# A delta-rule layer whose weight blocks come as two halves: head 1 to 7 by two GpSimd transfers and one ScalarE negative, in place of one transfer, one cast and one subtraction

## The chip, the cores and the metric

The kernel runs on one core of a Trainium2 chip. A core has five engines that run side by side, each through its own fixed list of instructions: TensorE (PE in the profile, with PEld for its weight loads), VectorE (DVE), ScalarE (ACT), GpSimd (POOL) and SyncE (SP, which here only issues transfers). Transfers run on 16 DMA engines; they are issued by SP into hardware queues, or by POOL into a software queue. The metric is the time of one execution on the device in microseconds (us), the median of several runs. The kernel before takes 1331.79 us (3 runs, 1331.76 to 1331.99).

## The reference

The reference is an encoder of two layers on x (1 x 512 x 1024), all in float32: a gated delta-rule layer, an MLP, a gated linear attention layer, an MLP, with a layer norm after each. Only the first of them is touched. Cut to that layer:

```python
def _mixer_gdn(h, w_in, conv_w, a_log, dt_bias, norm_g, w_out):
    proj = jnp.matmul(h, w_in).astype(F32)
    qkv = jax.nn.silu(_depthwise_conv(proj[..., :A_CONV_CH], conv_w.astype(F32)))
    z = proj[..., A_CONV_CH:A_CONV_CH + A_VW]
...
    q = _l2norm(heads(qkv[..., :A_W], A_DK)) * (A_DK ** -0.5)
    k = _l2norm(heads(qkv[..., A_W:2 * A_W], A_DK))
    v = heads(qkv[..., 2 * A_W:], A_DV)
...
    o_f = _gated_delta_chunked(q, k, v, beta[0], g[0])
    o_b = _flip(_gated_delta_chunked(_flip(q), _flip(k), _flip(v), _flip(beta[1]), _flip(g[1])))
    o = (o_f + o_b).transpose(0, 2, 1, 3)
    o = _rmsnorm(o, norm_g) * jax.nn.silu(z.reshape(bn, s, A_HEADS, A_DV))
    return jnp.matmul(o.reshape(bn, s, A_VW).astype(w_out.dtype), w_out)
```

There are 8 heads of width 128, so the projection has, for each head, four column blocks of w_in: k, q, v and z, each 1024 x 128.

## The kernel before, in words

**Three products for one.** A float32 matrix product is made from halves in a reduced format (fp32r in the profile): each operand is split into a high part, the value rounded to that format, and a low part, the rest. `mm3` (L122, L123, L124) adds high by high, low by high and high by low. A weight block is 128 x 1024 in the core's memory (8 slices of 128 rows of w_in side by side), and its projection is 24 matmuls of 128 x 512: L122, L123 and L124 for each of the 8 slices. The activations' halves xth and xtl are made once at the start and kept.

**How a weight block comes in before.** `wcols` (L104 to L111) takes a buffer `wst`, has SP load the block into it from device memory (`dma`, L50), and calls `split` (L84 to L102): ACT casts `wst` to the high part `wh` (L96), and DVE subtracts, `wl` = `wst` - `wh` (L101). The pool `wst` has 3 buffers; the pool `whl` has 3 buffers of `wh` and 3 of `wl`. So block n can be cast when the matmuls of block n-3 have read their halves, while the load into `wst` runs up to three blocks ahead of that.

`split` has another way (`by_dma`, L97 to L99), used at a few places of later stages: ACT writes the negative of the source into the low part, and a POOL transfer with an add accumulates a second copy onto it.

**Order.** `GdnHead.project` (from L1408) makes the four blocks of a head in the order k, q, v, z, and behind each the short convolution (`conv`, L1395 on ACT and L1399 four times on DVE) or, for z, a copy (L1434); behind q stands a silu over two or four tiles (L1437, with an activation table load ahead, and one behind at L55). `rows` (from L1446) transposes k and q (`ktp`, L1457, PE), copies the transposed k to `kt` (L1460), sums squares (`junk`, L1462, eight of them), takes the logarithm (`lnr`, L1465, ACT), makes scale factors on DVE and ACT (L1472 to L1498; `neg`, `kds`, `fq` on ACT), and has PE transpose the rows `rsp` to `rtp` (L1483). Then `solve` (the triangular inverse: `ep`, `kk`, `hp`, `lv`, `nw`, `xp`), `recur` (the two chunked recurrences: `m`, `op`) and `finish` (norm, gate, transpose) follow. The head's parts are generators: while head i projects, head i-1 solves and head i-2 recurs and finishes. A scheduler that models the engines draws from them and sets a fixed list for each engine; at run time every engine goes through its list in order, and an instruction that waits holds up all that stand behind it on the same engine. Priorities come out of the model, so an instruction that the model thinks late or early moves the others too.

Head 0 is special: its k block is loaded with the first transfers of the program, and its other three are issued early. While head 0 projects, POOL is still making masks (`blk`, `ic`, `icc`, `self`, `sel`, L1163 to L1205).

Of the kernel before, what the change touches and what calls it, by code (L numbers as in the profile page):

```python
# [8 lines left out]
F32 = mybir.dt.float32  # L9
F32R = mybir.dt.float32r  # L10
# [3 lines left out]
ALU = mybir.AluOpType  # L14
# [3 lines left out]
P = 128  # L18
# [10 lines left out]
class Ctx:  # L29
# [74 lines left out]
    def wcols(self, w, c0, n=P, pool=None, late=(), by_dma=False):  # L104

        st = self.wst.tile([P, KT, n], F32, name="wst", tag="wst")
        self.dma(st, w[c0 // n])
        with contextlib.ExitStack() as es:
            for i in late:
                es.enter_context(self.tc.issue_after(i.ins))  # L110
            return self.split(st, [P, KT, n], pool, by_dma)  # L111

    def wrows(self, w, r0, c0, pool=None):

        st = self.wst.tile([P, 2, 512], F32, name="wst", tag="wst")
        self.dma(st, w[r0 // (2 * P), c0 // 512])
        return self.split(st, [P, 2, 512], pool)
# [1253 lines left out]
class GdnHead:  # L1371
# [35 lines left out]
    def project(self, done):  # L1407

        c, pool, g, h = self.c, self.pool, self.g, self.h
        A = c.nc.scalar  # L1410
        if h == 0:
            self.new_tile()
        kq = self.kq
        for i, ci in enumerate((A_H + h, h, 2 * A_H + h, 3 * A_H + h)):
            if h == 0 and i == 0:
                ps = g.k0
            else:
                with g.then() if h == 0 else contextlib.nullcontext():
                    wh, wl = c.wcols(self.w_in, ci * P)
                ps = c.bank([P, S], F32, name="pj" + "kqvz"[i], tag="pj")  # L1420
                for k in range(KT):
                    c.mm3(ps, wh[:, k, :], wl[:, k, :], c.xth[:, k, :], c.xtl[:, k, :], k == 0, k == KT - 1)
                    if h == 0 and (i, k) == (3, 6):
                        g.sums()
                        yield from rows
                    if k < KT - 1:
                        yield 0.69, 0.0
            if i == 2:
                vz = self.next.new_tile()
                self.v, self.sz = vz[:, 0, :], vz[:, 1, :]  # L1430
            if i < 3:
                self.conv(kq[:, i, :] if i < 2 else self.v, ps, ci)
            else:
                A.copy(self.sz, ps)  # L1434
            if i == 1 or i == 3 and h == A_H - 1:
                t = vz if i == 3 else self.sil if h else kq
                c.exp_ln_after(A.activation(t, t, AF.Silu))  # L1437
            yield 0.69, 0.0
            if i == 1:
                rows = self.rows(done)  # L1440
                if h:
                    yield from rows
                else:
                    next(rows)
                    next(rows)
# [384 lines left out]
```

## Time and profile before

The profiled execution is one run out of several; its span is the time from its first to its last instruction.

| What | Value |
|---|---|
| median of 3 runs | 1331.79 us (1331.76 to 1331.99) |
| the profiled execution, its own time | 1330.95 us |
| its span | 1329.0 us |
| mean granted TensorE clock | 0.997 |
| delta-rule layer in the span | about 0 to 375 us, heads 1 to 7 projected from 37.5 to 333.3 us |

The profile's page gives, for each engine, busy time, share of the span and number of instructions, then the chain of work that ended last, then groups of instructions. A stage of the kernel is read from the view by windows: busy time of each engine in a stretch, the clock, the share of the 16 DMA engines in use, and GB/s. The timeline lists single instructions: start, duration, engine, line, output <- input, and in brackets the idle time ahead of it on that engine with what ended it. Matmuls overlap in PE's pipeline, so the time that one costs is the distance of two starts, not its duration.

### The profile page before, as it was taken

Reading aid. Unit: us, or ns where it says so; the run is one execution under the profiler, and the core shown is the slowest. Engines: PE = TensorE matmul, PEld = TensorE weight load, DVE = VectorE, ACT = ScalarE, POOL = GpSimd, SP = SyncE. Lnnn points to the kernel's source line nnn. Section 1 sums busy time; section 2 is a strip of 40 time slices with the busy share of each in tenths; the row PEclk is TensorE's granted clock in tenths of the full one; section 3 lists DMA queues with packets and bytes.
Section 4 is the critical chain, followed back from the end, with each engine's and each line's share of the span. In section 5 each row is a group of like instructions: output and inputs, shape, how many; then the busy total and the mean of one; then the engine's idle time right before and its main releaser. Section 6 shows DMA issues by size and latency. Waiting matters only on the chain.

```text
span 1329.0 us, 22303 instructions
## 1 busy us (share of the span) xinstructions
PE 1310.3 (99%) x8659; PEld 1120.2 (84%) x8659; DVE 1108.9 (83%) x1818; ACT 805.3 (61%) x1598; POOL 124.7 (9%) x177
## 2 busy tenths in 40 slices
PE   9999999999999999999999999999999999999996
PEld 7777877777877889999998888888889899999985
DVE  7787888878768988989988787867878789889888
ACT  4757666767643666566667754554466466566656
POOL 5000000000001810101101200000001001101011
PEclk9999999999999999999999999999999999999998
DMA  5210110111232574575548521211217365556465
GB/s 182 95 49 33 55 59 34 63 49 56 73 112 96 176 179 153 145 196 152 149 146 169 154 85 64 75 53 64 96 63 226 94 196 151 146 172 157 145 140 145
DMA packets 44044, 154.35 MB, mean 116 GB/s; under 512 B 5419, under 2 KB 5795, under 8 KB 43939
## 3 DMA queue, kind: packets, MB, share of 16 engines
q1 hardware_dynamic: 32163, 110.85, 24.6%
q0 software_dynamic: 11776, 42.08, 15.9%
q8 instruction: 68, 1.11, 0.3%
q14 instruction: 37, 0.30, 0.1%
HBM read 113.99 MB, written 2.10 MB: 87 GB/s over the span
## 4 chain that ended last, share of the span: by engine, by line
PE 92%; DVE 4%; ACT 3%; issue 1%; DVEq 0%; POOL 0%; ACTq 0%; POOLq 0%
PE fx L124 3%; PE fx L123 3%; PE fx L122 3%; PE pX L123 3%; PE pX L122 3%; PE pX L124 3%; PE pjv L122 3%; PE pjv L123 3%; PE pjv L124 3%; PE m L1692 3%; PE fyz L124 3%; PE fyz L122 3%; PE fyz L123 3%; PE pY L123 2%; PE pY L122 2%; PE pY L124 2%
## 5 line engine op out<-in xcount | busy, mean ns | idle before, releaser
L96 ACT CAST wh<-wst 128x1024 fp32r<-128x1024 f32 x152 | 159.5, 1049 | 115.9 <-PE fyz L123 38.2
L101 DVE TENSOR_TENSOR wl<-wst,wh 128x1024 fp32r<-128x1024 f32 x150 | 184.7, 1232 | 46.1 <-ACT wh L96 45.3
L101 DVE TENSOR_TENSOR w2l<-w2r,w2h 128x1024 fp32r<-128x1024 f32 x92 | 112.5, 1223 | 22.2 <-ACT w2h L96 22.2
L96 ACT CAST w2h<-w2r 128x1024 fp32r<-128x1024 f32 x94 | 98.4, 1048 | 45.1 <-PE pX L124 16.7
L400 POOL DMA_DIRECT2D w2r<-w2r x56 | 48.5, 896 | 497.4 <-DVE w2l L101 252.9
L96 ACT CAST ah<-h 128x1024 fp32r<-128x1024 f32 x56 | 58.9, 1051 | 40.4 <-PE pX L123 18.3
L448 DVE TENSOR_TENSOR wst<-wst 128x512 f32<-128x512 f32 x120 | 80.0, 688 | 0.4
L101 DVE TENSOR_TENSOR al<-h,ah 128x1024 fp32r<-128x1024 f32 x56 | 68.5, 1223 | 4.4 <-ACT ah L96 4.4
L123 PE MATMUL pX<-w2l,ah 128*128 128x512 f32 x168 | 66.2, 394 | 0.0
L122 PE MATMUL pX<-w2h,ah 128*128 128x512 f32 x168 | 66.1, 393 | 0.0
L124 PE MATMUL pX<-w2h,al 128*128 128x512 f32 x168 | 65.7, 391 | 0.0
L122 PE MATMUL pjv<-wh,xth 128*128 128x512 f32 x128 | 54.4, 425 | 0.0
L124 PE MATMUL fx<-xh,wl 128*128 128x256 f32 x192 | 54.3, 283 | 0.0
L124 PE MATMUL fyz<-xh,wl 128*128 128x256 f32 x192 | 54.2, 282 | 0.0
L122 PE MATMUL fx<-xth,wh 128*128 128x256 f32 x192 | 54.2, 282 | 0.0
L124 PE MATMUL fx<-xth,wl 128*128 128x256 f32 x192 | 54.2, 282 | 0.0
L123 PE MATMUL fx<-xtl,wh 128*128 128x256 f32 x192 | 54.2, 282 | 0.0
L122 PE MATMUL fyz<-xh,wh 128*128 128x256 f32 x192 | 54.2, 282 | 0.0
L123 PE MATMUL fx<-xl,wh 128*128 128x256 f32 x192 | 54.1, 282 | 0.0
L123 PE MATMUL fyz<-xl,wh 128*128 128x256 f32 x192 | 54.0, 281 | 0.0
L122 PE MATMUL fx<-xh,wh 128*128 128x256 f32 x192 | 53.8, 280 | 0.0
L123 PE MATMUL pj<-xtl,wh 128*128 128x256 f32 (+1 forms) x160 | 52.2, 328 | 0.2 <-DVE xtl L188 0.2
(536 smaller groups left out, 4326.2 us busy)
## 6 DMA issues: line engine op xcount, KB each, us to landing
wst<-in_w SPq DMA_DIRECT2D x68, 512.0 KB, 4.3
w2r<-in_w SPq DMA_DIRECT2D x60, 512.0 KB, 3.8
w2r<-w2r POOLq DMA_DIRECT2D x56, 512.0 KB, 5.3
wst<-in_a_in SPq DMA_DIRECT2D x32, 512.0 KB, 3.3
wst<-in_b_vr SPq DMA_DIRECT2D x16, 512.0 KB, 3.4
wst<-in_a_out SPq DMA_DIRECT2D x8, 512.0 KB, 3.3
wst<-in_b_in SPq DMA_DIRECT2D x8, 512.0 KB, 3.4
wst<-in_b_out SPq DMA_DIRECT2D x8, 512.0 KB, 3.3
```

The costliest lines, as they stand in the source:

```text
L96: h = nc.scalar.copy(hi, src)
L101: self.halves = h, nc.vector.tensor_tensor(lo, src, hi.bitcast(F32), ALU.subtract)
L122: mm(ps, ah, bh, start=start, stop=False, **kw)
L123: mm(ps, ah, bl, start=False, stop=False, **kw)
L124: self.last_mm = mm(ps, al, bh, start=False, stop=stop, **kw)
L400: nc.gpsimd.dma_start(blocks[a + (q,)], blocks[b + (q,)], accum_op=ALU.add)
L448: plus = lambda a, b: V.tensor_tensor(a, a, b, ALU.add)
L1692: T.matmul(ps[:, d, :], *ops(d), start=True, stop=True)
```

## The change

A new function `wcast` makes the two halves without `wst`: POOL issues a transfer from device memory into `wh` whose type is fp32r, so the transfer rounds; ACT writes the negative of `wh` into `wl`; POOL issues a second transfer of the same block from device memory, which adds to `wl`. `project` uses it for the blocks of heads 1 to 7 (28 blocks); head 0 keeps `wcols`. The lines behind it move down by 9: L1395 becomes L1404, and so on; `mm3` becomes L131 to L133.

```diff
+    def wcast(self, src):
+
+        nc = self.nc
+        hi, lo = (self.whl.tile(list(src.shape), F32R, name=n, tag=n) for n in ("wh", "wl"))
+        nc.gpsimd.dma_start(hi, src)
+        nc.scalar.mul(lo, hi.bitcast(F32), -1.0)
+        nc.gpsimd.dma_start(lo, src, accum_op=ALU.add)
+        return hi, lo
...
@@ GdnHead.project
                 with g.then() if h == 0 else contextlib.nullcontext():
-                    wh, wl = c.wcols(self.w_in, ci * P)
+                    wh, wl = c.wcast(self.w_in[ci]) if h else c.wcols(self.w_in, ci * P)
                 ps = c.bank([P, S], F32, name="pj" + "kqvz"[i], tag="pj")
```

The lists of the engines change at many places, since the scheduler is run anew. SP loses 28 loads, DVE loses 28 subtractions, ACT has 28 negatives in place of 28 casts, POOL gains 56 transfers, PE has the same matmuls in a slightly other order. Behind the delta-rule layer the lists are the same but for small shifts near its end. Two places are shown.

**The first block of head 1.** POOL's list before, at the end of its masks (`ic`, `icc`, `self` and `sel` are masks; the next row belongs to the layer norm at the end of the layer):

```order
L1203 TENSOR_TENSOR ic<-ic 128x4
L1205 CAST icc<-ic 128x4
L1163 MEMSET self 6x256
L1165 AFFINE_SELECT self<-self 6x256 x3
L1168 CAST sel<-self 6x256
L213 DMA lnp<-in_ln_g 128x512 x2
```

And in the changed kernel at the same place:

```order
L1212 TENSOR_TENSOR ic<-ic 128x4
L1214 CAST icc<-ic 128x4
L117 DMA wh<-in_a_in 128x1024
L1172 MEMSET self 6x256
L1174 AFFINE_SELECT self<-self 6x256 x3
L1177 CAST sel<-self 6x256
L119 DMA wl<-in_a_in 128x1024
L117 DMA wh<-in_a_in 128x1024 x2
L119 DMA wl<-in_a_in 128x1024 x2
```

The first transfer of a high part stands behind the mask `icc`, and the first of a low part behind the mask `sel`; from there on high and low alternate, at four spots two and two as in the last two rows.

ACT's list before, while head 0 projects (`ge` is of the gates, `sil` holds what the convolutions make, the third row is head 1's first block):

```order
L1279 ACTIVATE ge<-ge 128x128
L96 CAST wh<-wst 128x1024
L1395 ACTIVATE sil<-pjq,cw 128x512
L1437 ACT_TABLE_LOAD
L1437 ACTIVATE sil<-sil 128x1024
L55 ACT_TABLE_LOAD
L1460 COPY kt<-ktp 128x512
```

And in the changed kernel:

```order
L1288 ACTIVATE ge<-ge 128x128
L1404 ACTIVATE sil<-pjq,cw 128x512
L118 ACTIVATE wl<-wh 128x1024
L1446 ACT_TABLE_LOAD
L1446 ACTIVATE sil<-sil 128x1024
L55 ACT_TABLE_LOAD
L1469 COPY kt<-ktp 128x512
```

The negative of head 1's k block stands directly ahead of the table load and the silu of head 0, behind whose result head 0's transposes `ktp` stand on PE; the cast that it replaces stood one row further up.

On PE, behind the end of head 0's z projection, the second group of `ktp` stands behind 5 matmuls of head 1's k block (6 before), and `rtp` behind 18 of them (24 before).

**Head 2's rows, while head 3 projects.** ACT's list before (`ssp` gets the sums of squares that `lnr` takes, `pjz` is the z projection of head 2, `oss` belongs to head 1's finish, `pz` to head 2's solve):

```order
L96 CAST wh<-wst 128x1024
L1740 ACTIVATE junk,oss<-op 128x128
L1462 ACTIVATE junk,ssp<-ktp 128x128 x4
L96 CAST wh<-wst 128x1024
L1465 ACTIVATE lnr<-ssp,bias_77 128x8
L1434 COPY sil<-pjz 128x512
L1612 CAST pz_135<-lv 32x4x32 x4
L1489 ACTIVATE neg<-rw 128x8
```

And in the changed kernel:

```order
L118 ACTIVATE wl<-wh 128x1024
L1443 COPY sil<-pjz 128x512
L1749 ACTIVATE junk,oss<-op 128x128
L1471 ACTIVATE junk,ssp<-ktp 128x128 x2
L118 ACTIVATE wl<-wh 128x1024
L1471 ACTIVATE junk,ssp<-ktp 128x128 x2
L205 ACTIVATE rsy<-oss,bias_77 128x4
L1474 ACTIVATE lnr<-ssp,bias_77 128x8
L206 ACTIVATE rsy<-rsy 128x4
L1498 ACTIVATE neg<-rw 128x8
```

The negative of head 3's v block (the second L118) stands ahead of the last two sums of squares and of `lnr`, and the `pz` casts of the solve, which stood between `lnr` and `neg`, stand further up.

PE's list before, ahead of the `rtp` of head 2 (`ath`, `Dd` and `lv` belong to head 2's solve):

```order
L1598 LDWEIGHTS ath
L1598 MATMUL lv<-Dd,ath 128x64
L122 MATMUL pjk<-xth,wh 128x512
L123 MATMUL pjk<-xtl,wh 128x512
L124 MATMUL pjk<-xth,wl 128x512
L1483 LDWEIGHTS rsp
L1483 MATMUL rtp<-idb,rsp 6x128
```

And in the changed kernel:

```order
L132 MATMUL pjk<-xtl,wh 128x512
L133 MATMUL pjk<-xth,wl 128x512
L131 MATMUL pjk<-xth,wh 128x512
L132 MATMUL pjk<-xtl,wh 128x512
L1492 LDWEIGHTS rsp
L1492 MATMUL rtp<-idb,rsp 6x128
```

In the changed kernel the `lv` products of head 2 stand earlier, ahead of the end of head 2's z projection. From the last matmul of that projection to `rtp` there are now 4 transposes `ktp`, 4 products `qk`, 8 products `nw` and 17 projection matmuls of head 3's k block.

## The prediction

> **What bounds the kernel now.** I read first the engines' shares and the chain that ended last, on the page:
>
> ```profile
> PE 1310.3 (99%) x8659; PEld 1120.2 (84%) x8659; DVE 1108.9 (83%) x1818; ACT 805.3 (61%) x1598; POOL 124.7 (9%) x177
> PE 92%; DVE 4%; ACT 3%; issue 1%; DVEq 0%; POOL 0%; ACTq 0%; POOLq 0%
> ```
>
> PE sets the end. The change lies in the delta-rule layer, so the view by windows comes next, for the start, the stretch where heads 1 to 7 project, and the end of the layer (PE, PEld, DVE, ACT, POOL busy, clock, DMA share, GB/s):
>
> ```profile
> 0.00:36.00 36.00, 33.82 (x166) 27.79 (x166) 26.16 (x52) 18.89 (x28) 17.25 (x47) 1.00 0.52 181
> 36.00:330.00 294.00, 291.42 (x2543) 231.43 (x2542) 245.56 (x514) 198.70 (x564) 0.00 (x0) 1.00 0.16 54
> ```
>
> From 36 to 330 us PE is idle for 294.00 - 291.42 = **2.6 us**, at full clock, with the DMA engines at 16%. Nothing else is full: DVE has 48 us to spare, ACT 95, POOL does nothing. So whatever the change takes off DVE or SP can win little, and whatever makes PE wait counts in full. What PE waits for in this layer (us, times, longest):
>
> ```profile
> PE lv L1598 <- ACT pz L1612: 1.7, 6, 0.4
> PE nw L1644 <- ACT Dd L1633: 0.8, 2, 0.6
> PE ktp L1457 <- ACT sil L1437: 0.7, 1, 0.7
> PE ktp L1457 <- ACT junk L1462: 0.4, 1, 0.4
> ```
>
> PE waits for ACT, never for a weight. Against the durations that PE's matmuls have at their closest spacing the layer also holds a few us more that no row names; I count them neither way.
>
> **The change part by part.** Removed from DVE, and what ACT's cast waits for now (us, times):
>
> ```profile
> L101 DVE TENSOR_TENSOR wl<-wst,wh x28: 1209/1218/1227, 39.5 to 315.9; 128x1024 fp32r<-128x1024 f32 x28
> ...
> L96 ACT CAST wh<-wst x29: 1034/1047/1137, 35.9 to 327.7; 128x1024 fp32r<-128x1024 f32 x29
> its engine sat idle before it (us, times) until:
>   PE pjv L123: 9.4, 3
>   PE pjk L123: 7.7, 5
> ```
>
> DVE is relieved of 28 x 1.218 = 34.1 us. PE's 2.6 us of idle is the most that this can return; its named waits are for ACT, which feeds on DVE at one remove, so I take **-1.0** (bounds 0 and -2.6). PE has the same matmuls, in an order with 12 fewer changes between a projection and something else. A matmul of 128x512 costs 0.23 us behind its like and 0.31 behind another kind (starts 39.25, 39.56, 39.79 below), so 12 x 0.08 = **-1.0**.
>
> ACT keeps an instruction of the same length: the negative takes what the cast took (the row of a like one below, 1051 against 1047 ns). But the cast waited only until PE freed a buffer, since its `wst` had landed long before; the rows above show it standing for PE, 9.4 and 7.7 us in all, at no cost to PE. The negative waits until PE frees the buffer **and** a POOL transfer into it has landed. ACT stands longer by one landing, with all that is queued behind the negative. That is the price to size. Landings of 512 KB (median us from issue), the POOL instruction that issues one, and a negative of the same shape:
>
> ```profile
> wst<-in_a_in SPq DMA_DIRECT2D x32, 512.0 KB, 3.3
> w2r<-w2r POOLq DMA_DIRECT2D x56, 512.0 KB, 5.3
> wl<-wst POOLq DMA_DIRECT2D x2, 512.0 KB, 4.9
> ln<-in_ln_b POOLq DMA_DIRECT2D x2, 512.0 KB, 4.1
> ...
> L400 POOL DMA_DIRECT2D w2r<-w2r x56: 847/859/1245, 460.8 to 1285.2; - x56
> ...
> L98 ACT ACTIVATE wl<-wst x2: 1048/1051/1054, 731.3 to 738.2; 128x1024 fp32r<-128x1024 f32 x2
> ```
>
> No row shows a rounding transfer. Plain ones from SP take 3.3, accumulating ones of POOL 5.3, a plain one of POOL from device memory 4.1. The last is the nearest, same queue and same source, so the landing is **4.1**, with 3.3 and 5.3 kept as ends. In a sentence apart: the Trainium skill, page "DMA: Bandwidth & Descriptors", section "Anatomy of one DMA — SWDGE (gpsimd) path", fits 2.0 us plus bytes over 436 GB/s to a POOL transfer, an estimate of 3.2 us for 512 KB; the trace's 4.1 to 5.3 doesn't agree, and by 3.2 each place below would cost 0.9 less.
>
> The weights themselves come in time. A block's buffer is free when the block three before it ends; landing, negative, second landing are 4.1 + 1.05 + 4.9 = 10 us, and the blocks themselves start 13 us (head 1) to 28 us after that (starts of `pjk`, `pjq`, `pjv`, `pjz` in the timeline). L124, the only reader of `wl`, comes third. So PE should wait for ACT, not for weights.
>
> **Term 1, the start.** POOL, ACT and PE in the timeline:
>
> ```profile
> 28.42 0.19 POOL L1205 CAST icc<-ic 128x4 f16<-128x4 f32 x1
> ...
> 30.69 1.28 ACT L1437 ACT_TABLE_LOAD   x1 [4.73 <-DVE sil L1399]
> 31.98 1.06 ACT L1437 ACTIVATE sil<-sil 128x1024 f32<-128x1024 f32 x1
> 41.19 0.30 ACT L1465 ACTIVATE lnr<-ssp,bias 128x8 f32<-128x8 f32 x1
> ...
> 33.09 0.66 PE L1457 MATMUL ktp<-ident,sil 128*128 128x128 f32 x4 [0.65 <-ACT sil L1437]
> 43.53 0.39 PE L1483 MATMUL rtp<-idb,rsp 128*6 128x128 bf16 x4
> ```
>
> Head 1's first transfer stands behind `icc`, so it is issued at 28.6 and lands at 32.7; the negative ends at 33.8, the table load and the silu 1.28 + 1.06 later at 36.1. PE's `ktp`, which waits for that silu already, started at 33.09 with the silu's end at 33.04. **+3.1** (3.3: +2.3; 5.3: +4.3). Nothing on PE can slip in: in PE's list `ktp` keeps its place.
>
> **Term 2, head 0's rows.** In PE's new list `rtp` of head 0 stands behind 18 matmuls of head 1's k block in place of 24, the second `ktp` behind 5 in place of 6. From F, the end of head 0's z projection, PE has 18 matmuls and a `ktp` to `rtp`: 18 x 0.23 + 2 x 0.08 + 0.36 = 4.7 us. The second `ktp` is done at F + 1.6, its four sums of squares and `egl` put `lnr` at F + 3.5, and from `lnr` to the last row cast on DVE it is 43.12 - 41.19 = 1.9 (rows above and below): F + 5.4. PE waits 0.7 to 0.9: **+0.8**. The negative of head 1's v block stands behind `lnr`; it ends at F + 0.2 + 4.1 + 1.05 = F + 5.4, and `neg`, `kds`, `fq` (0.65) bring ACT to `rt` at F + 6.0, when `rtp` is done too: nothing more at 4.1, up to 1.2 at 5.3.
>
> ```profile
> 42.95 0.17 DVE L1480 CAST rsp<-r 128x8 bf16<-128x8 f32 x1
> ```
>
> **Term 3, the later heads.** The costliest place is head 2's rows, where the negative of head 3's v block now stands among the sums of squares. Let F be the end of head 2's z projection on PE. ACT: landing 4.1, negative 1.05, two sums of squares of 0.40 (starts 39.99, 40.40), `rsy` 0.3, and the 1.9 from `lnr` to the last row cast: 8.2 us. PE from F to `rtp`: 4 `ktp` 0.36, 4 `qk` 1.0, 8 `nw` 0.46, 17 matmuls 17 x 0.23 + 2 x 0.08 = 4.1: 5.9 us.
>
> ```profile
> 38.89 0.60 PE L1457 MATMUL ktp<-ident,sil 128*128 128x128 f32 x4
> 39.25 0.47 PE L122 MATMUL pjk<-xth,wh 128*128 128x512 f32 x1
> 39.56 0.39 PE L123 MATMUL pjk<-xtl,wh 128*128 128x512 f32 x1
> 39.79 0.39 PE L124 MATMUL pjk<-xth,wl 128*128 128x512 f32 x1
> ...
> 120.50 1.16 PE L1651 MATMUL qk<-sil 128*128 128x128 f32 x8
> 121.50 0.38 PE L1750 MATMUL otp<-ident,fo 128*128 128x128 f32 x2
> ...
> 122.38 0.39 PE L1666 MATMUL nw<-Xd,a 128*128 128x128 f16 x4
> 122.61 0.44 PE L1512 MATMUL kk<-sil 128*128 128x128 f32 x2
> ...
> 39.99 0.28 ACT L1462 ACTIVATE junk<-ktp 128x128 f32<-128x128 f32 x1
> ...
> 40.40 0.27 ACT L1462 ACTIVATE junk<-ktp 128x128 f32<-128x128 f32 x1
> ```
>
> PE waits 2.3 us. Without the landing ACT would still need `ktp` from PE (done at F + 1.9), all four sums (1.6), the negative, `rsy` and the 1.9, together 6.7, so 0.8 of it comes from the new order; at the later heads the order makes such tight spots and removes others, and I charge only what the landing adds, 8.2 - 6.7 = **1.5**. The same sum at the other 25 blocks, each with the instructions between the negative and the next ACT result that PE waits for, gives 0 at 19, and at six 1.15 (q of head 4), 0.3 (v of 4), 1.1 (v of 5), 0.8 (k of 6), 0.7 (q of 6) and 0.6 (v of 6), together **4.7**; these six are estimates, from rows of the same kinds as those shown. At 3.3 the seven places shrink to about 2.5 in all; at 5.3 each costs 1.2 more, and a few new ones appear: about 17.
>
> **The sum.** 3.1 + 0.8 + 1.5 + 4.7 - 1.0 - 1.0 = **+8.1 us**. The profiled execution took 1330.95 with a span of 1329.0, so it would be 1339.1; the runs' median is 0.8 above it, and the forecast for a median is **1340**. The ends of the unknown landing: 3.3 gives 2.3 + 0.8 + 2.5 - 2 = +3.6, 1335, and a DVE relief at its bound, -2.6, 1334; 5.3 gives 4.3 + 2.0 + 17 - 1 = +22, 1354.
>
> **The rivals.**
>
> (A) *The waits are hidden and the relief counts* (the other side). ACT has 95 us to spare, and the order that I read row by row may let PE run on while ACT stands. Then only the gains stay: -1.0 and at most -2.6, so 1328 to 1331. It decides if the first rounding transfer lands by 29.6, since then the silu isn't late; at 28.6 issued, no row has a landing that short. Against it too: PE's four rows of waits are all for ACT.
>
> (B) *A rounding transfer lands like an accumulating one or later.* Each word is changed on the way, as in an accumulation, and two POOL transfers of one block share the queue. At 5.3 or more it is the upper end, 1350 to 1356. For it speaks that the accumulating rows are the only ones of POOL that do arithmetic; against it, that DMA is at 16% here.
>
> (C) *POOL issues late.* If DVE holds POOL up while it writes a transfer's descriptors, each place is late by that: the 56 issues of the row above take 847 to 1245 ns beside a DVE as busy as here, so at most 0.4 us at the seven places and the start, +3.2, 1343. The Trainium skill, page "SBUF — State Buffer", section "Who interferes with whom", says that DVE in a two-port mode fully blocks GpSimd, and that a POOL transfer can starve so; the median of 859 against a least of 847 shows almost none of it here.
>
> (D) *The transfer doesn't round.* Then `wl` would be zero, with the same instructions and waits: the time is that of the forecast.
>
> **How the numbers follow.** A measurement of this kernel can tell about 0.2%, 2.7 us, from no change: faster is below 1329.1, slower above 1334.5. The forecast, with landings of 3.5 to 5.0 and with (C) and (D) in it, 1335 to 1349: 0.60, slower. (B), 1350 to 1356: 0.12, slower. (A), 1328 to 1331: 0.16, of it 0.10 faster and 0.06 the same. That the places cost less than I sum, since PE waits once for what I count twice, 1331 to 1335: 0.12, the same but for 0.01. So slower 0.73, same 0.17, faster 0.10. The range 1330 to 1355 leaves out most of (A) and the last of (B), somewhat under 2 in 10.
>
> **What would show it.** Right: `ktp` of head 0 on PE waits 3 to 4 us for the silu; ACT's idle time ahead of L118 is put down to the DMA of `wh` and sums to well over the 21 us that L96 stood; PE's idle time in 36 to 330 grows from 2.6 to about 10, at waits for ACT (`rt`, `pz`, `qd`, `junk`); the transfer of `wh` lands in 4.1. Term 1 is wrong if `ktp` starts before 35. It is all wrong if PE waits for `wl` itself (a second landing far over 5 us, or POOL's order holding a transfer back), or if PE's busy time rather than its idle time changes.

## The result, and the profile after

| | us, median (range, runs) |
|---|---|
| before | 1331.76 (1331.29 to 1331.99, 5) |
| changed | 1343.72 (1341.89 to 1346.42, 5) |
| ratio, changed to before | 1.0093, 95% interval 1.0082 to 1.0104 |

The change makes the kernel slower by 12 us, 0.9%. The profiled execution of the changed kernel is the median run: 1343.72 us, span 1342.0 (before: 1330.95, span 1329.0). Its page, part 1, against the line shown of before:

```profile
PE 1315.1 (98%) x8659; PEld 1122.4 (84%) x8659; DVE 1081.6 (81%) x1790; ACT 807.8 (60%) x1598; POOL 165.6 (12%) x233
```

PE is busy for 4.8 us more (1315.1 against 1310.3) though it has the same 8659 matmuls, and idle for 8.2 us more (1342.0 - 1315.1 = 26.9 against 18.7). Together these are the 13.0 us of the two spans: not only waits, but slower matmuls too. All but 0.5 of it is lost in the delta-rule layer: the first matmul of the MLP behind it starts at 430.9 us in place of 418.4, and from there to the end it is 911.1 against 910.6. (The layer reaches to that matmul, and not only to about 375 us as the table ahead of the change has it.)

The stretch from 36 to 330 us in the same columns as above (PE, PEld, DVE, ACT, POOL busy, clock, DMA share, GB/s):

```profile
36.00:330.00 294.00, 286.56 (x2407) 226.46 (x2408) 209.37 (x472) 194.29 (x542) 37.99 (x54) 0.99 0.47 104
```

PE is idle there for 7.4 us, against 2.6 before.

What PE waits for, in the first 400 us (total, times, longest):

```profile
PE ktp L1466 <- ACT sil L1446: 4.4, 2, 4.1
PE lv L1607 <- ACT pz L1621: 2.2, 3, 1.3
...
PE ktp L1687 <- ACT rt L1494: 1.4, 1, 1.4
PE hp L1562 <- DVE a L1551: 1.3, 1, 1.3
PE nw L1653 <- ACT Dd L1642: 0.9, 3, 0.4
PE rtp L1492 <- DVE rsp L1489: 0.3, 1, 0.3
```

Four single waits of over 1 us carry most of the idle time: 4.1 at head 0's silu, and 1.3, 1.4 and 1.3. Before has none over 0.7 there, apart from one of 1.5 at the very start of the program that both have. The group of the negatives in ACT's list, between 30 and 345 us:

```profile
L118 ACT ACTIVATE wl<-wh x28: 1045/1060/1142, 33.1 to 314.1; 128x1024 fp32r<-128x1024 f32 x28
its engine sat idle before it (us, times) until:
  DMA wh<-in_a_in: 38.7, 17
```

The cast it replaces took as long (1047 ns), and waited for PE only. Now ACT stands 38.7 us, in 17 of 28 places, for the rounding transfer. Landings of the two transfers on the page, part 6 (median us from issue):

```profile
wh<-in_a_in POOLq DMA_DIRECT2D x28, 512.0 KB, 3.7
wl<-in_a_in POOLq DMA_DIRECT2D x28, 512.0 KB, 5.4
```

The start, in the timeline of ACT and PE:

```profile
33.10 1.06 ACT L118 ACTIVATE wl<-wh 128x1024 fp32r<-128x1024 f32 x1 [7.79 <-DMA wh<-in_a_in]
34.18 1.28 ACT L1446 ACT_TABLE_LOAD   x1
35.47 1.06 ACT L1446 ACTIVATE sil<-sil 128x1024 f32<-128x1024 f32 x1
...
36.58 0.82 PE L1466 MATMUL ktp<-ident,sil 128*128 128x128 f32 x4 [4.06 <-ACT sil L1446]
37.06 0.77 PE L133 MATMUL pjz<-xth,wl 128*128 128x512 f32 x1
37.63 0.63 PE L131 MATMUL pjz<-xth,wh 128*128 128x512 f32 x1
```

The chain is the one that was forecast: landing, negative, table load, silu, transposes. But behind the wait two projection matmuls start 0.57 us apart, and later ones 0.43, where before had 0.23. The granted clock tells why (the view by windows; PE busy is the first number behind the length, the clock stands ahead of the last two):

```profile
30.00:36.50 6.50, 2.52 (x12) 1.75 (x10) 2.81 (x8) 3.37 (x3) 3.43 (x7) 1.00 0.38 91
36.50:37.00 0.50, 0.42 (x4) 0.42 (x5) 0.00 (x0) 0.48 (x2) 0.00 (x0) 0.94 0.83 98
37.00:40.00 3.00, 3.00 (x10) 2.42 (x9) 0.69 (x1) 2.52 (x7) 0.00 (x0) 0.50 1.00 243
40.00:40.50 0.50, 0.50 (x2) 0.36 (x2) 0.06 (x1) 0.00 (x0) 0.00 (x0) 0.65 1.00 369
...
60.50:61.00 0.50, 0.50 (x11) 0.33 (x9) 0.41 (x1) 0.00 (x0) 0.00 (x0) 0.83 0.98 188
61.00:64.00 3.00, 3.00 (x9) 2.35 (x8) 2.86 (x5) 0.00 (x0) 0.00 (x0) 0.50 0.95 268
64.00:64.50 0.50, 0.50 (x3) 0.43 (x2) 0.00 (x0) 0.11 (x1) 0.00 (x0) 0.76 0.00 0
```

After the wait of 4.1 us PE runs at **half clock** for some 3.4 us, and once more from 60.7 to 64.2, some 2 us behind the wait of 1.3 at 57.6. Each stretch costs 3.0 x 0.5 and its two edges, 1.7 us, an estimate from the clock's column. Before had the full clock all through the layer.

The Trainium skill, page "TensorE: Matmul & The Clock Gate", section "Part 1: The HAM clock gate", has the array's clock at half after about one idle window of some 3.4 us. The first stretch agrees (4.1 us idle). The second doesn't: 1.3 us idle, with some narrow matmuls behind it, was enough.

### The profile page after: what moved, and what is told of

It reads as the page before. It is cut to its first block, busy times and chain, and to the rows that moved or that the text cites. A ratio compares the mean times of both kernels' runs of the same rounds, so it can differ in the third digit from the quotient of the medians.

```text
span 1342.0 us, 22329 instructions
## 1 busy us (share of the span) xinstructions
PE 1315.1 (98%) x8659; PEld 1122.4 (84%) x8659; DVE 1081.6 (81%) x1790; ACT 807.8 (60%) x1598; POOL 165.6 (12%) x233
## 4 chain that ended last, share of the span: by engine, by line
PE 64%; DVE 3%; ACT 1%; issue 0%; DVEq 0%; POOL 0%; POOLq 0%; ACTq 0%
PE fx L133 3%; PE fx L132 3%; PE fx L131 3%; PE pX L132 3%; PE pX L131 3%; PE pX L133 3%; PE fyz L133 3%; PE fyz L131 3%; PE fyz L132 3%; PE pY L132 2%; PE pY L131 2%; PE pjv L133 2%; PE pjv L131 2%; PE pjv L132 2%; PE pY L133 2%; PE scp L997 2%
## 5 line engine op out<-in xcount | busy, mean ns | idle before, releaser
L96 ACT CAST wh<-wst 128x1024 fp32r<-128x1024 f32 x124 | 129.9, 1048 | 89.5 <-PE fyz L132 39.6
L101 DVE TENSOR_TENSOR wl<-wst,wh 128x1024 fp32r<-128x1024 f32 x122 | 150.5, 1234 | 40.2 <-ACT wh L96 39.2
L96 ACT CAST w2h<-w2r 128x1024 fp32r<-128x1024 f32 x94 | 98.3, 1047 | 44.2 <-PE pX L133 16.7
L132 PE MATMUL pX<-w2l,ah 128*128 128x512 f32 x168 | 66.2, 394 | 0.0
L131 PE MATMUL pX<-w2h,ah 128*128 128x512 f32 x168 | 66.1, 393 | 0.0
L133 PE MATMUL pX<-w2h,al 128*128 128x512 f32 x168 | 65.7, 391 | 0.0
L131 PE MATMUL pjv<-wh,xth 128*128 128x512 f32 x128 | 54.4, 425 | 0.0
L133 PE MATMUL fx<-xh,wl 128*128 128x256 f32 x192 | 54.3, 283 | 0.0
L131 PE MATMUL fx<-xth,wh 128*128 128x256 f32 x192 | 54.2, 282 | 0.0
L133 PE MATMUL fyz<-xh,wl 128*128 128x256 f32 x192 | 54.2, 282 | 0.0
L132 PE MATMUL fx<-xtl,wh 128*128 128x256 f32 x192 | 54.2, 282 | 0.0
L133 PE MATMUL fx<-xth,wl 128*128 128x256 f32 x192 | 54.2, 282 | 0.0
L131 PE MATMUL fyz<-xh,wh 128*128 128x256 f32 x192 | 54.2, 282 | 0.0
L132 PE MATMUL fx<-xl,wh 128*128 128x256 f32 x192 | 54.1, 282 | 0.0
L132 PE MATMUL fyz<-xl,wh 128*128 128x256 f32 x192 | 54.0, 281 | 0.0
L131 PE MATMUL fx<-xh,wh 128*128 128x256 f32 x192 | 53.8, 280 | 0.0
L118 ACT ACTIVATE wl<-wh 128x1024 fp32r<-128x1024 f32 x28 | 29.8, 1065 | 38.7 <-DMA wh<-in_a_in 38.7
```

What stands on the lines that cost most here:

```text
L96: h = nc.scalar.copy(hi, src)
L101: self.halves = h, nc.vector.tensor_tensor(lo, src, hi.bitcast(F32), ALU.subtract)
L118: nc.scalar.mul(lo, hi.bitcast(F32), -1.0)
L131: mm(ps, ah, bh, start=start, stop=False, **kw)
L132: mm(ps, ah, bl, start=False, stop=False, **kw)
L133: self.last_mm = mm(ps, al, bh, start=False, stop=stop, **kw)
```

## The experiments

The theory: the loss comes from one combination, the negative on ACT that has to wait for the rounding transfer's landing, with what is queued behind it. The rivals: the adding transfers and the traffic; the new order of the lists as such. Every kernel was timed beside before, 5 or 11 times, and before's medians there were 1331.0 to 1331.4. The scheduler is run anew for each edit, so each of these kernels also has lists of its own. Ratios are to before, with the 95% interval.

**e8: the start alone.** Only head 1's k block comes the new way.

```diff
-                    wh, wl = c.wcast(self.w_in[ci]) if h else c.wcols(self.w_in, ci * P)
+                    wh, wl = c.wcast(self.w_in[ci]) if h == 1 and i == 0 else c.wcols(self.w_in, ci * P)
```

> Only head 1's k block comes by the two transfers and the negative, the other 27 the old way. Theory: the silu of head 0 waits for the first landing as in the change, PE idles 4.1 us in place of 0.7, and runs at half clock for 3.4 us behind it: 1331.4 + 3.4 + 1.7 = 1336.5 (1335.5 to 1338). If the half clock is not due to the idle time, 1334.8; if the start is made up later, under 1333.

Measured: 1336.55 us, ratio 1.0038 (1.0025 to 1.0051), within the range. PE's longest wait, and then the clock behind it (windows):

```profile
PE ktp L1466 <- ACT sil L1446: 3.8, 1, 3.8
```

```profile
36.00:37.00 1.00, 0.98 (x5) 0.98 (x6) 0.00 (x0) 1.00 (x1) 0.00 (x0) 0.63 0.82 135
37.00:39.00 2.00, 2.00 (x6) 1.52 (x6) 0.25 (x1) 1.99 (x8) 0.00 (x0) 0.50 0.83 162
39.00:40.00 1.00, 1.00 (x5) 0.79 (x4) 0.49 (x1) 1.00 (x3) 0.00 (x0) 0.66 0.00 0
```

One block of 28 costs 5.1 us. Of it the trace shows 3.82 - 0.65 = 3.2 of waiting, and 0.37 + 1.0 + 0.34 = 1.7 at the lower clock, together 4.9. The wait alone would have given 1334.6.

**e1: all but the start.** The mirror image: `h > 1 or h and i` in place of `h`, so head 1's k block comes the old way.

> Head 1's k block comes the old way (SP load, ACT cast, DVE subtraction); the other 27 blocks keep the two transfers. Theory (ACT stands in front of the silu until the first rounding transfer lands, PE then idles 4.1 us and runs 3.4 us at half clock): head 0's transposes wait under 1 us again, no half clock between 36 and 42 us, and the time falls by 3.4 + 1.7 = 5.1 us from 1343.7 to 1338.6 (1337 to 1340). If the half clock had nothing to do with the idle time, only 3.4 come back, 1340.3. Rival (the loss is spread over the layer, by the new order or by the added traffic, and the start is made up later anyway): 1342.5 to 1345.

Measured: 1339.47 us (1337.58 to 1342.78), ratio 1.0067 (1.0054 to 1.0079): 4.3 less than the change, within the range. The wait at the silu is 0.7 again, and the clock is 1.00 between 36 and 42 us. But a stretch of lower clock stands at another place now, behind the wait for `rt`, here 1.35 us long:

```profile
36.00:42.00 6.00, 6.00 (x34) 4.96 (x32) 4.19 (x16) 4.38 (x19) 1.51 (x2) 1.00 0.55 115
216.00:217.00 1.00, 1.00 (x8) 0.70 (x7) 0.00 (x0) 0.86 (x5) 0.47 (x1) 1.00 0.00 0
217.00:220.00 3.00, 3.00 (x13) 2.43 (x14) 2.39 (x4) 2.98 (x8) 0.00 (x0) 0.65 0.99 158
220.00:221.00 1.00, 1.00 (x6) 0.66 (x5) 0.41 (x2) 0.01 (x1) 0.00 (x0) 0.50 0.27 49
```

In the changed kernel the wait of 1.4 at that very place brought no such stretch. So the same wait can come with the 1.7 us or without. The scatter of the changed kernel points the same way (4.5 us over five runs, against 0.7 of before): from its fastest run to its slowest the mean granted clock of the whole run goes 0.996, 0.995, 0.994, 0.994, 0.994, and that of e1 goes 0.997, 0.996, 0.996, 0.995, 0.995. One stretch is worth 1.7 / 1342 = 0.0013 of it. Which wait had a stretch behind it is known for the one traced run of each only.

**e5: the rounding transfer without the negative and the adding transfer.**

```diff
+        st = self.wst.tile(list(src.shape), F32, name="wst", tag="wst")
+        self.dma(st, src)
         nc.gpsimd.dma_start(hi, src)
-        nc.scalar.mul(lo, hi.bitcast(F32), -1.0)
-        nc.gpsimd.dma_start(lo, src, accum_op=ALU.add)
+        nc.vector.tensor_tensor(lo, st, hi.bitcast(F32), ALU.subtract)
```

> Only the first part of the change: the high part by the rounding transfer, the low part by an SP load and DVE's subtraction as before; no negative, no adding transfer. ACT loses the 30 us of casts, DVE stands in the wait for the landing. Theory (the landing of the rounding transfer is the price, the adding transfer comes in time anyway): within 1.5 us of the run with the negative on DVE. Rival (the adding transfers, 5.4 us each in the same queue, are what costs): at least 3 us faster than that run, and at or below the time of before.

**e4: the negative and the adding transfer without the rounding transfer.** `c.wcols(self.w_in, ci * P, by_dma=h > 0)`: ACT casts as before, then writes the negative, and the transfer adds the block that lies in `wst`, so that no block is read from device memory twice.

> Only the second part of the change: SP load and ACT's cast for the high part as before, then ACT's negative of the loaded block and an adding transfer from the loaded block (inside the chip). ACT works 30 us more, and waits for no landing ahead of the negative. Theory (the rounding transfer's landing in front of ACT is the main loss): PE waits for no more than some 6 us in the layer, 1331 to 1335. Rival (adding transfers and their issue order cost as much as the landing): 1338 or more.

Measured: e5 1331.38 us, ratio 1.0000 (0.9991 to 1.0009); e4 1332.39 us, ratio 1.0008 (0.9999 to 1.0017). Page, part 1, of e5 and then of e4:

```profile
PE 1311.1 (98%) x8659; PEld 1122.9 (84%) x8659; DVE 1110.3 (83%) x1818; ACT 780.6 (59%) x1570; POOL 140.7 (11%) x205
```

```profile
PE 1310.3 (98%) x8659; PEld 1119.1 (84%) x8659; DVE 1081.6 (81%) x1790; ACT 830.9 (62%) x1626; POOL 150.1 (11%) x205
```

**Either half of the change by itself costs nothing that can be told from zero.** e5 has the same 28 rounding transfers, and DVE stood 5.3 us for them; e4 has 28 negatives and 28 adding transfers, and 26 us more of ACT. The loss comes with both: ACT's instruction behind a landing. (These two have lists of their own too, and other edits below lose several us by theirs, so a good order may have helped here; no run tells.) They also say what relief is worth: 25 us less on ACT (e5) and 27 less on DVE (e4) gave nothing.

**e3: the negative on DVE.** `nc.vector.tensor_scalar_mul` in place of `nc.scalar.mul`.

> The negative is made by DVE in place of ACT; transfers as in the change. Theory (what counts is which engine stands in the wait, and what is queued behind it): ACT never waits for a transfer, loses 30 us of work, and PE's waits for ACT go away; DVE, with 80 us to spare, stands in the wait, and its convolutions, which have some us of slack, take most of it: 1332 to 1338. Rival (any engine in front of PE does the same harm): 1341 to 1346, with PE's waits now for DVE.

Measured: 1335.65 us, ratio 1.0035 (1.0022 to 1.0047), within the range, and 8 us less than the change with the same transfers. ACT no longer waits for a rounding transfer; DVE stands 7.8 us for them. Three of PE's waits are new:

```profile
PE xp L1578 <- DVE Dd L1569: 1.1, 1, 1.1
PE pjz L133 <- DMA wl<-in_a_in: 0.9, 1, 0.9
PE pjk L133 <- DMA wl<-in_a_in: 0.8, 1, 0.8
```

Here the weights themselves come late, twice, by 1.7 us together: that much of the 4.2 us over before is the adding transfers' landing. The run is 4.3 above e5, where the theory had the two within 1.5 of each other; the rival, that the adding transfers are the difference, forecast this gap. The next two test that.

**e6 and e7: without the adding transfers,** with the negative on ACT (e6) and on DVE (e7). The line `nc.gpsimd.dma_start(lo, src, accum_op=ALU.add)` is taken out of `wcast`.

> The change without its adding transfers: the low part stays the negative of the high part (the sum with the block is left out), so POOL issues only the 28 rounding transfers and PE waits for ACT's negative alone. Theory (ACT's wait for the landing of the rounding transfer is the main loss): ACT still idles over 30 us ahead of the negatives, and the time stays at 1341 to 1344.5. Rival (the adding transfers are the main loss, 4.3 us between the runs with the negative on DVE and with the subtraction): 1337 to 1340.

> Negative on DVE, and the adding transfers left out as above. If the 4.3 us between the negative on DVE (1335.7) and the subtraction (1331.4) are the adding transfers and their landings (PE waited 1.7 us for wl in two places, and for DVE results elsewhere), this takes 1330 to 1333. If they are the scheduler's order or the place of the DVE operation, 1334.5 to 1337.

Measured: e6 1341.91 us, ratio 1.0079 (1.0065 to 1.0093); 1.8 less than the change, with intervals that overlap: the adding transfers cost about 2 us or nothing. ACT idles 30.4 us for `wh`, PE waits 3.9 at the silu. The theory holds here. e7 took 1338.54 us, ratio 1.0054 (1.0042 to 1.0067): *more* than e3 with the transfers, outside both expectations. PE's longest waits in e7 are of another kind:

```profile
PE lv L1606 <- DVE pz L1615: 1.2, 1, 1.2
PE nw L1652 <- ACT Dd L1641: 1.1, 3, 0.4
PE ob L130 <- ACT oh L1765: 1.0, 1, 1.0
...
PE ob L334 <- DVE xt L244: 0.7, 1, 0.7
PE pj L130 <- ACT xth L195: 0.7, 1, 0.7
```

The last three stand at the very end of the layer (410 to 424 us), 100 us behind the last weight block: e7's list has the output projection in an order that leaves PE waiting there. Between 400 and 435 us PE is idle for 3.4 us in e7, and for none in before, in the change and in e6. No weight block is near, so this is put down to the scheduler's order, and it hides what e7 was to show. So e4 and e6 show that the adding transfers aren't the main loss beside a negative on ACT; what they cost beside one on DVE stays open but for the 1.7 us of e3.

**e2: no landing in front of ACT.** Every other high part goes into a buffer of `wst`, so that six are in use and the transfers can start a block earlier.

```diff
-        hi, lo = (self.whl.tile(list(src.shape), F32R, name=n, tag=n) for n in ("wh", "wl"))
+        self.alt = 1 - getattr(self, "alt", 0)
+        hi = (self.wst.tile(list(src.shape), F32R, name="wst", tag="wst") if self.alt else
+              self.whl.tile(list(src.shape), F32R, name="wh", tag="wh"))
+        lo = self.whl.tile(list(src.shape), F32R, name="wl", tag="wl")
```

> The same transfers and negatives, but every other high part goes into a buffer of the pool wst, so that there are six buffers for high parts in place of three, and a rounding transfer is issued about a block (7 us or more) earlier. Theory (ACT's wait for the landing is the loss): ACT's idle time ahead of the negative that is put down to a DMA falls from 38.7 us to under 5, PE's waits go back to about 4 us, and the time is within 2.5 us of before, 1330 to 1334. Rival 1 (traffic: twice the bytes from device memory, half of them accumulated, slow something down): the transfers are all there, so 1340 or more. Rival 2 (the scheduler's new order as such): 1336 to 1342, with PE waits left that are not behind a negative.

Measured: 1337.02 us, ratio 1.0043 (1.0030 to 1.0055): 6.7 less than the change, but 5.6 over before. ACT never idles for a rounding transfer any more (38.7 us before this edit, none now), and no stretch is at a lower clock; still the time isn't that of before, and falls where the rival on the order had it. 1.5 us are at the start: PE waits 2.1 us at the silu in place of 0.65, since the silu is late once more, by another road. Timeline of e2, POOL and DVE:

```profile
20.82 2.11 POOL L1205 TENSOR_TENSOR off<-blk 128x512 f16<-128x512 f32 x1
...
25.05 1.30 POOL L1205 TENSOR_TENSOR off<-blk 128x512 f16<-128x512 f32 x1
...
28.81 1.27 POOL L1205 TENSOR_TENSOR off<-blk 128x512 f16<-128x512 f32 x1
...
21.69 1.32 DVE L1293 TENSOR_SCALAR gd<-ge 128x128 f32<-128x128 f32 x1
...
25.36 1.15 DVE L1296 TENSOR_TENSOR gd<-ge 128x128 f32<-128x128 f32 x1
...
28.89 1.34 DVE L1300 SCALAR_TENSOR_TENSOR gl<-gl,gd 128x128 f32<-128x128 f32 x1
```

Each of these DVE instructions starts while the POOL instruction beside it runs and ends about when that ends. In before the same three took 0.27 to 0.35 us. But before has two such places of its own, beside its `off` instructions at 19.50 and 25.11 us:

```profile
19.83 2.04 DVE L101 TENSOR_TENSOR wl<-wst,wh 128x1024 fp32r<-128x1024 f32 x1
...
25.44 1.05 DVE L1286 TENSOR_SCALAR gl<-gd 128x128 f32<-128x128 f32 x1
```

The first takes 1.22 elsewhere, the second 0.21 in e2. So before loses some 1.7 us in this way, and e2 some 2.9: the transfers among POOL's masks have moved these into other DVE instructions and cost 1.2 us more. Head 0's convolutions stand behind them on DVE, and the table load ahead of the silu starts at 32.89 us in place of 30.69; what makes up the rest of these 2.2 us was not followed. The Trainium skill, page "SBUF — State Buffer", section "Who interferes with whom", gives DVE and GpSimd a shared pair of memory ports that one holds against the other for a whole instruction; these rows agree, with GpSimd as the holder.

Two more pieces of the other 4 us can be named in the trace. PE waits for `Dd` six times, 2.5 us in all, where before had 0.8 in two; at 75.4 us, for one, `Dd` stands behind a negative that waited for nothing but took its 1.07 us. And at the end of the layer, between 400 and 435 us and far from any weight block of a head, PE is idle for 1.7 us, before for none. (The waits for `pz`, 1.8 us, are as long as in before, 1.7.) From 36 to 330 us PE's idle time is 4.8 us: 7.4 in the change, 2.6 in before.

**e9: six buffers, and head 1's k block the old way.**

> Six buffers for high parts and head 1's k block the old way: neither the start nor a landing in front of ACT is left, but 27 rounding transfers, 27 negatives and 27 adding transfers are. With six buffers alone it was 1337.0, of which 1.5 us were PE's longer wait for head 0's silu. If the rest, some 4 us, is the new order of the lists (small waits all over the layer), 1334.5 to 1336.5. If landings in front of ACT and the start are the whole loss, 1330.5 to 1333.

Measured: 1340.32 us, ratio 1.0069 (1.0057 to 1.0082), above both ranges. The wait at the silu is down from 2.1 to 1.0, but the layer's end has the same waits as e7's (`oh` 1.0, `xt` 0.8, `xth` 0.7): PE is idle for 3.4 us between 400 and 435, and from 412.5 to 416.5 us the clock is at about half, which costs 1.7. So 5.1 of the 9.3 us over before lie where no weight block comes in. Taking away two causes brought a worse order.

**e10: the same instructions in another order.** In before, `run(new.project(done))` is written ahead of `run(mid.solve(done))`. The program writes out head i-2's recurrence, head i-1's solve and head i's projection one after another, each to its end, and the scheduler sets the lists from that sequence (so the generators are not drawn from in turn in this layer, as the section on the kernel before may be read).

> The kernel before with one edit that changes no instruction: head i's projection is written ahead of head i-1's solve, so that the scheduler makes other lists from the same work. It shows what an order alone is worth. If orders of the scheduler differ by several us, 1333.5 to 1338; if they are worth little, 1330.5 to 1332.5, and the rest of the loss must come from the transfers.

Measured: 1366.77 us, ratio 1.0270 (1.0256 to 1.0284), with no instruction added or taken away. This edit moves whole parts of a head, so it gives no size for the others; it shows that an order of this scheduler can cost three times the whole change. A third of it is the clock: three stretches at 0.50, of 6.7, 10.2 and 6.9 us, cost some 12 of the 38 us between the spans. Two of them start among waits of PE of about 0.5 us each, one after another.

## Why the prediction was right

Slower was forecast, 1340 with a range of 1330 to 1355; it is 1343.7. The reason, ACT standing in front of a landing while PE comes to need what is queued behind, is what the runs show for the main part: e8 and e1 give the start 5.1 and 4.3 of the 12 us, e4 and e5 hold the two halves apart and lose nothing, and e3, with DVE in ACT's place, loses a third. The number came this close in part by luck, since errors of 3 to 4 us on both sides cancel (below). Of the signs that the prediction named, `ktp` waits 4.06 us (3 to 4 forecast), and ACT stands 38.7 us for `wh` (well over 21); PE's idle time from 36 to 330 us grew to 7.4 and not to about 10, and PE's busy time grew by 4.8 us, which it had named as a sign against itself had it come in place of idle time: 3.4 of that is the clock. By its steps:

- **What bounds the kernel** held: 25 to 27 us less on ACT or DVE gave nothing (e4, e5). The two gains in the sum, -1.0 for DVE's relief and -1.0 for fewer changes between kinds of matmuls, did not come. PE does change kinds 12 times less, but its busy time beyond the half clock rose by some 1.4 us; why is not shown.
- **The landing**, 4.1 taken, is 3.7 for the rounding transfer, and 5.4 for the adding one (4.9 taken). So rival (B) is out. In a sentence apart: the 3.2 us that was worked out from the Trainium skill's page "DMA: Bandwidth & Descriptors", section "Anatomy of one DMA — SWDGE (gpsimd) path", is short of both.
- **Term 1, the start**, +3.1, is the one that was mis-sized. The wait is right: 4.06 - 0.65 = 3.4 in the changed kernel, 3.2 in e8. But the term left out that PE comes back at half clock: +1.7, so 5.1 for the start (e8, and 4.3 by e1).
- **Term 2, head 0's rows**, +0.8: a wait of 0.3, on DVE's `rsp` as forecast.
- **Term 3, the later heads**, 1.5 + 4.7, was right in kind, and right at two of seven places: q of head 4 (forecast 1.15, measured 1.3 at `pz`) and v of head 5 (1.1, measured 1.4 at `rt`). In both ACT had just waited for `wh`, 0.5 and 2.1 us, so that at the first the landing is less than half of PE's wait, and the rest is the negative's own 1.06 us in that place of the list:

```profile
161.06 1.06 ACT L118 ACTIVATE wl<-wh 128x1024 fp32r<-128x1024 f32 x1 [0.53 <-DMA wh<-in_a_in]
162.14 1.06 ACT L1621 CAST pz<-lv 32x128 f16<-32x128 f32 x4
...
219.33 1.06 ACT L118 ACTIVATE wl<-wh 128x1024 fp32r<-128x1024 f32 x1 [2.14 <-DMA wh<-in_a_in]
220.29 0.56 ACT L1494 COPY rt<-rtp 6x512 bf16<-6x512 bf16 x1
```

A third place, z of head 1, was costed at nothing and cost 1.3 (a negative that waited 1.6 us ahead of `ath`, behind which DVE's `a` and PE's `hp` stand), and 1.7 more by the half clock behind it. The other five places cost nothing, or 0.2 at most. The worked example, v of head 3: its transfer was issued at 121.63 us, 0.9 ahead of the block's last matmul, and ACT came to the negative at 125.50 with no wait. The step took the buffer to be free with the last matmul of the block; the high part is last read by L132, and the landing came out 0.4 shorter.

So of 13.0 us between the two spans: start 3.4, the three places 3.9, `rsp` 0.3, two stretches of half clock 3.4, together 11.0. The other 2 are 0.6 of small waits and the 1.4 of busy time. Against the forecast's 8.1 us, the clock (3.4), the place that wasn't seen (1.3), the gains that didn't come (2.0) and these last 2 us were missing, and the start and the two places ran 0.7 over. On the other side five places didn't cost their 3.9, and `rsp` 0.5 less than its 0.8.

What stays open is how much of the 7 us beside the start would come back in the *same* order without the landing. Every edit that takes the landing away makes the scheduler write other lists, and those kernels still lose 4 us (e2) and 9 (e9) beside their starts, a good part of it at the layer's end. A run with the order held fixed was not tried.

## What to carry to other kernels

An instruction of the same length isn't the same if it waits for something else: a cast whose input lay ready has become a negative behind a transfer, and an engine that is 60% busy stops the one that is 99% busy. So when a producer moves to a transfer, look at what is queued behind its consumer, put the consumer on the engine with the least urgent queue (8 of the 12 us came back in e3) or start the transfer a buffer earlier (6.7 in e2), and change one half at a time, since here each half alone was free. Price a wait of TensorE with the clock behind it: the 3.4 us at the start cost 5.1. And before a difference of a few us is put down to an edit, look where in the trace it lies: e2, e7 and e9 lost 1.7 to 5.1 us at the layer's end, where nothing of the edit runs.

## What was not expected of the hardware

- A wait of TensorE of 3.8 to 4.1 us was followed by some 3.4 us at a granted clock of 0.50 in all three kernels whose profile shows such a wait (the change, e6, e8). Waits of 1.3 to 1.4 us were followed by it in some cases (57.6 us in the change, 216 us in e1), and not in others (163 and 220 us in the change), and one of 2.2 us wasn't either (161 us in e6). In e9 it came among waits of at most 1.0 us, and in e10 stretches of 6.7 and 10.2 us came among waits of about 0.5 us each. So the length of one wait does not decide it, and what does is not shown here.
- The issue of a rounding transfer held POOL for 0.55 us in the median, that of an adding one for 0.87.
- DVE instructions of 0.3 us took 1.15 to 1.34 in e2 beside POOL's `off` instructions, whose placement the transfers had changed; in before one of 0.2 took 1.05 in the same way.
